# Moving layer 0's modulation vectors from the vector engines to TensorE, and packing the weights by block

## The chip, the cores and the metric

The kernel runs on one core of one Trainium2 chip. The metric is device microseconds of a whole launch. Before the change the median of three runs is 1066.75 us (1066.24 to 1068.56).

## The reference, cut to what matters

The model is a two-layer trunk for 256 tokens of 1024 features, all in float32. Every layer has three sub-layers: a feed-forward network (FFN), a token mixer, and a second FFN. Before each of them the input is modulated by a shift and a scale, and the output of each is weighted by a gate. These nine vectors per layer come from one conditioning vector by a matrix-vector product:

```python
cond = jax.nn.silu(c)                       # (1, 1024)
for l in range(DEPTH):                      # 2 layers
    mod = cond @ ada_w[l] + ada_b[l]        # ada_w[l]: 1024 x 9216, 36 MiB
    sh1, sc1, gt1, sh2, sc2, gt2, sh3, sc3, gt3 = jnp.split(mod, N_MOD, axis=-1)
    f1 = swiglu(modulate(x, sh1, sc1), ffn1_w1[l], ffn1_w3[l], ffn1_w2[l])
    x = layer_norm(DEEPNORM_ALPHA * x + MACARON_HALF * gt1[:, None, :] * f1, ln_g[l, 0], ln_b[l, 0])
    m = token_mixer(modulate(x, sh2, sc2), ...)      # LRU, retention, state-space heads
    x = layer_norm(DEEPNORM_ALPHA * x + gt2[:, None, :] * m, ln_g[l, 1], ln_b[l, 1])
    f2 = swiglu(modulate(x, sh3, sc3), ffn2_w1[l], ffn2_w3[l], ffn2_w2[l])
    x = layer_norm(DEEPNORM_ALPHA * x + MACARON_HALF * gt3[:, None, :] * f2, ln_g[l, 2], ln_b[l, 2])
```

`modulate` is `x * (1 + scale) + shift`; an FFN has w1 and w3 of 1024 x 2816 and w2 of 2816 x 1024.

## The kernel before, in words

**Matrix products.** Every weight block is loaded in float32 into one of three `raw` buffers (128 x 2048). ScalarE (ACT) rounds a half of it, 128 x 1024, to the reduced form fp32r (`wh`), VectorE (DVE) subtracts to get what was lost (`wl`), and the activations are split likewise (`xTh`, `xTl`). A product is then three fp32r matmuls (`mm3`): high by high, high by low, low by high. There are 8 `wh` and 8 `wl` buffers.

**Modulation vectors before.** A vector pair or quadruple is made by `ada_group`. Each item of it loads two chunks of `ada_w` (128 x 1024, rows of 4 KiB) into `s4` buffers, which the profile shows as `s_slot`. One chunk is multiplied by a condition column and added on DVE in one instruction (`scalar_tensor_tensor` in `add_cond`); the other is scaled on ACT and added by DVE. After the last item DVE adds both sums, PE transposes them and DVE reduces over the partitions. Layer 0's vectors 2 to 5 are made in the background of its first FFN, 6 and 7 (`late`) at that FFN's end and the mixer's start. Vector 8 and the vectors of layer 1 come later, in the same manner.

**The start.** `begin` makes the first two vectors (shift 1 and scale 1) together with the first FFN's first columns, in four sections of 256 features. A section loads its part of `ada_w` in pieces of 128 x 4 x 256 (rows of 1 KiB), 256 columns of x, and weights of w1 and w3. DVE and ACT do the 16 multiply-adds of 128 x 256 (`G_SHARE` of them on ACT with an add on DVE), PE transposes the result, DVE and ACT modulate x into `xTh` and `xTl`, and PE does 36 matmuls of 512 columns for the section. Two of a section's three pieces of weights are recorded together with the next section (`LATE`).

**What sets the order.** Nothing is in program order. `Scheduler` records all operations, gives each an estimated duration (`cost`) and a latest start (`place_late`), and places them by list scheduling (`run`), each engine in one fixed order. DMA loads are all issued by SP, also in one fixed order, so that a load waits behind those ahead of it when their buffer is not yet free. The profile shows one source line for all instructions (the one that emits them), so tiles tell them apart. Operations within `sch.fused()` stay together: in the mixer, `y_mm` uses it for four matmuls of 32 output columns each, which go to the four column tiles of the array and stand in the profile as `r_slot<-s_slot,CT`. Each such float32 matmul stands in the trace as two records; an fp32r matmul stands as one.

**Stages.** By the layer norms' statistics in the trace, layer 0's first FFN ends at 225.1 us, its mixer at 357.7, its second FFN at 548.4; layer 1's at 748.5, 870.4 and 1055.5.

Of the kernel before, what the change touches and what calls it, by code (L numbers as in the profile page):

```python
# [66 lines left out]

FFN_SLOTS = 21
# [6 lines left out]
SMB = 8  # L75
# [127 lines left out]
class Scheduler:  # L203
# [156 lines left out]
    def cost(self, eng, m, a, k, out, ins, n, fs, scal, psum, op):  # L360
        if eng == E_SPQ:
# [4 lines left out]
            op.nbytes = nb if run >= 512 else max(2 * nb, nb // run * 157)  # L366
# [286 lines left out]
def trunk_kernel(ctx: ExitStack, tc: tile.TileContext, a: dict, cst: bass.AP, out: bass.AP):  # L653
# [46 lines left out]
    cond = {n: cp.tile([128, KD * n], F32, name=f"cond{n}") for n in (1, 2, 4)}  # L700
    hpi = cp.tile([128, 1], F32, name="hpi")
# [67 lines left out]
    def rows_k(w, r0, r1, c0, c1):  # L769
        return w[r0:r1, c0:c1].rearrange("(k p) f -> p k f", p=128)  # L770

    def piece(w, r0, r1, c0, c1, nm, eng=None, by_cols=False):
        merge = "p k i f -> p k (i f)" if by_cols else "p i k f -> p (i k) f"
        p = Piece((r1 - r0) // 128, c1 - c0, lambda raw: [(raw.rearrange(merge), rows_k(w, r0, r1, c0, c1))], nm, by_cols)
        for i in range(2):
            p.convert(i, eng or V)
        return p
# [44 lines left out]
    def ada_group(vecs, ring=False):  # L822
# [49 lines left out]
        def gate_row(l, j):  # L872
            pt = bank(f"gtt{l}_{j}")
            PE.transpose(pt[0:32, 0:128], modFM[:, l, j:j + 4, :].rearrange("p j k -> p (j k)"), ident)
            row = small([32, 128], f"gtr{l}_{j}")
            S.mul(row, pt[0:32, 0:128], 1.0 if j == 5 else 0.5)
            gtd[l, j // 3] = dp.tile([D], F32, name=f"gtd{l}_{j}")
            SP.dma_start(gtd[l, j // 3].rearrange("(k p) -> k p", p=128), row[0:8, :])

        return [lambda q=q: item(q) for q in range(4 * n)]  # L880
# [110 lines left out]
    def ffn(l, s, nxt, last_features, bg, todo, start=None, late=None):  # L991
        w1, w3, w2 = [a[f"ffn{1 if s == 0 else 2}_{n}"][l] for n in ("w1", "w3", "w2")]
# [311 lines left out]
    def mixer(l, P, nxt, last_features, bg):  # L1304
        win, wout = a["mix_w_in"][l], a["mix_w_out"][l]
# [424 lines left out]
    G_SHARE = [4, 5, 5, 5]  # L1730

    def begin(hs):
        w1, w3 = a["ffn1_w1"][0], a["ffn1_w3"][0]
# [4 lines left out]
        cond_columns(1)  # L1738
        ada_bias_transpose()
# [3 lines left out]
        for n, (k0, nk) in enumerate(SECTIONS):  # L1743
            f0, f1 = k0 * 128, (k0 + nk) * 128
            raws = []
            for j in range(2):
                for q in range(2):
                    raw = t4([128, 4, f1 - f0], f"adaf{n}{j}{q}")
                    SP.dma_start(raw, rows_k(a["ada_w"][0], q * 512, q * 512 + 512, j * D + f0, j * D + f1))
                    raws += [raw[:, k, :] for k in range(4)]  # L1750
# [65 lines left out]
        for n in (2, 4):  # L1816
            cond_columns(n)
# [65 lines left out]
```

## Time and profile before

| | us |
|---|---|
| median of 3 runs | 1066.75 |
| the profiled execution | 1063.61 |
| its span | 1061.8 |
| PE busy | 989.6 (93%) |
| DVE busy | 898.2 (85%) |
| ACT busy | 571.4 (54%) |
| DMA moved | 260.85 MB, 246 GB/s over the span |

The profile shows one execution. A stretch is read by the busy time of each engine in it: an engine that is busy for the whole stretch bounds it, and where none is, the wait that ends last does. A matmul's duration runs from its issue to its end and overlaps with the next one's, so the cost of one on PE is the distance between two starts, not the duration. PEclk is the granted share of TensorE's clock: 1.00 is 2.4 GHz and 0.50 is 1.2 GHz.

### The profile page before, as it was taken

The numbers are of one execution on the slowest core, as the hardware profiler recorded it, in microseconds if no ns is written. First come the engines' busy times: TensorE is split into PE (matmuls) and PEld (weight loads), VectorE is DVE, ScalarE is ACT, GpSimd is POOL, SyncE is SP. The second block draws the span as 40 slices with busy tenths as digits, with TensorE's granted clock in tenths as the row PEclk, the third lists the DMA queues.
The fourth block names the chain that finished last, engine by engine and source line by source line (L and its number), as shares of the span: only waits on it lengthen the run. The fifth ranks groups of instructions, "written<-read, shape, count | busy, mean of one in ns | idle before, by whom it ended". The sixth has DMA issues, their size and how long they took to land. (4 is left out here: it accounts for less than half of the span.)

```text
span 1061.8 us, 16775 instructions
## 1 busy us (share of the span) xinstructions
PE 989.6 (93%) x6617; PEld 887.0 (84%) x6617; DVE 898.2 (85%) x1391; ACT 571.4 (54%) x739; POOL 34.8 (3%) x46
## 2 busy tenths in 40 slices
PE   4899999988699899999989989999998799999996
PEld 3688998978588699899968979998897578999995
DVE  7988999999999999999899996556999898555555
ACT  4676765554376565665556544443546655444440
POOL 0000000010001100000000000000000110000000
PEclk9999999989899999999999999999999899999999
DMA  9999999978138699999969995654460657565521
GB/s 313 313 378 340 348 368 341 334 234 250 41 127 283 227 333 357 381 385 339 335 241 330 328 325 161 199 185 131 137 211 9 229 164 244 189 198 193 180 104 40
DMA packets 159055, 260.85 MB, mean 246 GB/s; under 512 B 14464, under 2 KB 115328, under 8 KB 158976
## 3 DMA queue, kind: packets, MB, share of 16 engines
q1 hardware_dynamic: 158976, 259.77, 71.1%
q8 instruction: 52, 0.85, 0.3%
q14 instruction: 27, 0.22, 0.1%
HBM read 257.10 MB, written 1.07 MB: 243 GB/s over the span
## 5 line engine op out<-in xcount | busy, mean ns | idle before, releaser
L643 ACT CAST wh_slot<-raw_slot 128x1024 fp32r<-128x1024 f32 x320 | 330.8, 1049 | 288.2 <-PE r_slot L643 168.9
L643 DVE TENSOR_TENSOR wl_slot<-raw_slot,wh_slot 128x1024 fp32r<-128x1024 f32 x320 | 386.6, 1221 | 106.9 <-ACT wh_slot L643 105.2
L643 PE MATMUL r_slot<-xTh,wh_slot 128*128 128x256 f32 x1216 | 343.0, 282 | 3.6 <-DVE xTh L643 1.6
L643 PE MATMUL r_slot<-xTl,wh_slot 128*128 128x256 f32 x1216 | 341.5, 281 | 1.3 <-DVE xTl L643 1.2
L643 PE MATMUL r_slot<-xTh,wl_slot 128*128 128x256 f32 x1216 | 341.0, 280 | 0.0
L643 PEld LDWEIGHTS r_slot<-xTh,wh_slot 128*128 128x128 f32 x1216 | 229.6, 189 | 8.0 <-ACT s_slot L643 3.0
L643 PEld LDWEIGHTS r_slot<-xTh,wl_slot 128*128 128x128 f32 x1216 | 232.6, 191 | 0.0
L643 PEld LDWEIGHTS r_slot<-xTl,wh_slot 128*128 128x128 f32 x1216 | 229.8, 189 | 2.7 <-DVE xTl L643 1.7
L643 PE MATMUL r_slot<-wh_slot,g_slot 128*128 128x512 f32 x704 | 224.6, 393 | 0.9 <-DVE g_slot L643 0.9
L643 PE MATMUL r_slot<-wh_slot,xTh 128*128 128x512 f32 (+1 forms) x416 | 148.4, 359 | 11.3 <-DVE xTh L643 4.7
L643 PEld LDWEIGHTS r_slot<-wh_slot,g_slot 128*128 128x128 f32 x704 | 132.3, 189 | 27.3 <-DVE g_slot L643 1.5
L643 DVE TENSOR_TENSOR s_slot<-s_slot,s_slot 128x256 f32<-128x256 f32 (+6 forms) x211 | 147.1, 721 | 8.1 <-ACT s_slot L643 4.7
L643 PE MATMUL r_slot<-wl_slot,xTh 128*128 128x512 f32 (+1 forms) x416 | 146.8, 354 | 3.2 <-DVE wl_slot L643 3.2
L643 PE MATMUL r_slot<-wh_slot,xTl 128*128 128x512 f32 (+1 forms) x416 | 146.0, 353 | 1.6 <-DVE xTl L643 1.4
L643 PE MATMUL r_slot<-wl_slot,g_slot 128*128 128x512 f32 x352 | 138.4, 394 | 0.0
L643 ACT ACTIVATE s_slot<-s_slot,cond 128x1024 f32<-128x1024 f32 (+1 forms) x83 | 82.2, 1002 | 61.8 <-DMA s_slot<-in_ada_w_dram 58.4
L643 PEld LDWEIGHTS r_slot<-wh_slot,xTh 128*128 128x128 f32 x416 | 81.3, 196 | 24.4 <-DVE xTh L643 5.5
L643 DVE SCALAR_TENSOR_TENSOR s_slot<-s_slot,cond,s_slot 128x1024 f32<-128x1024 f32 (+1 forms) x96 | 93.7, 981 | 3.4 <-DMA s_slot<-in_ada_w_dram 3.2
L643 PEld LDWEIGHTS r_slot<-wh_slot,xTl 128*128 128x128 f32 x416 | 81.1, 195 | 14.6 <-DVE xTl L643 4.7
L643 PEld LDWEIGHTS r_slot<-wl_slot,xTh 128*128 128x128 f32 x416 | 81.1, 195 | 13.8 <-DVE wl_slot L643 4.4
L643 DVE TENSOR_TENSOR s_slot<-r_slot,s_slot 128x512 f32<-128x512 f32 x100 | 68.2, 688 | 20.5 <-PE r_slot L643 19.9
L643 PEld LDWEIGHTS r_slot<-wl_slot,g_slot 128*128 128x128 f32 x352 | 66.5, 189 | 12.3
(119 smaller groups left out, 656.8 us busy)
## 6 DMA issues: line engine op xcount, KB each, us to landing
raw_slot<-in_ffn_w_dram SPq DMA_DIRECT2D x126, 1024.0 KB
s_slot<-in_ada_w_dram SPq DMA_DIRECT2D x144, 512.0 KB
raw_slot<-in_mix_w_in_dram SPq DMA_DIRECT2D x20, 1024.0 KB
raw_slot<-in_mix_w_out_dram SPq DMA_DIRECT2D x8, 1024.0 KB
raw_slot<-in_ffn_w_dram SPq DMA_DIRECT2D x12, 512.0 KB
s_slot<-gtd SPq DMA_DIRECT2D x6, 512.0 KB
s_slot<-in_ln_g_dram SPq DMA_DIRECT2D x6, 512.0 KB
s_slot<-in_ln_b_dram SPq DMA_DIRECT2D x6, 512.0 KB
```

The source lines that it names most:

```text
L643: real(*[self.place(v) for v in a], **{n: self.place(v) for n, v in k.items()})
```

## The change: TensorE makes layer 0's vectors 0 to 7, and the host lays the weights out by block

The condition vector is laid 32 times side by side (`condrep`, 128 x 8 x 32), as the stationary operand of one column tile. In `ada_matmul`, which replaces `ada_group` for the vectors 2 to 7 of layer 0, four chunks of `ada_w` are one fused item of 16 float32 matmuls: for each of the four chunks, four of 256 columns, one on each column tile. Two items make a vector. ACT then copies the sums from PSUM, PE transposes them twice and DVE adds the bias. In `begin`, a section's 16 multiply-adds become eight float32 matmuls of 512 columns, on four column tiles, two deep; the four tiles hold different quarters of the contraction dimension and are added up by the reduction that stood there before. Vector 8 of layer 0 and all of layer 1's stay on DVE and ACT.

The host copies w1, w3, w2, the mixer's input and output weights, and the start's part of `ada_w` into one array, in which each block stands as it lies in the buffer: each partition's row is one run of 4 or 8 KiB. Before, a block of w1, w3 or the mixer's input weights had rows of 1 or 2 KiB, and one of w2 or the output weights rows of 4 KiB. The other loads of `ada_w` are as before, rows of 4 KiB. The planner's cost takes 6% off for runs of 4 KiB and more, and there are 6 instead of 8 small buffers (`SMB`).

```diff
+def _blocks():
...
+            if l == 0 and i == 1:
+                f0 = 1024
+                for n in range(4):
+                    for q in range(4):
+                        out.append([("ada_w", 0, q * 256 + k * 128, q * 256 + k * 128 + 128, j * D + n * 256, j * D + n * 256 + 256)
+                                    for k in range(2) for j in range(2)])
+                    out.append([(w, 0, n * 256, n * 256 + 256, 0, 512) for w in (w1, w3)])
+                    out.append([(w1, 0, n * 256, n * 256 + 256, 512, 1024)])
...
-SMB = 8
+SMB = 6
...
-            op.nbytes = nb if run >= 512 else max(2 * nb, nb // run * 157)
+            op.nbytes = nb * (0.94 if run >= 4096 else 1) if run >= 512 else max(2 * nb, nb // run * 157)
...
+    condrep = cp.tile([128, KD, 32], F32, name="condrep")
...
-    def rows_k(w, r0, r1, c0, c1):
-        return w[r0:r1, c0:c1].rearrange("(k p) f -> p k f", p=128)
+    where, _ = _packed()
+
+    def block(*parts):
+        n = sum((r1 - r0) * (c1 - c0) for _, _, r0, r1, c0, c1 in parts) // 128
+        return a["pack"][where[parts]:where[parts] + 128 * n].rearrange("(p f) -> p f", p=128)
...
+    def ada_matmul(l, j):
+
+        nm = f"{l}_{j}"
+        raws = []
+        box = {}
+
+        def item(q):
+            for k in range(2):
+                raws.append(t4([128, D], f"adaw{nm}_{2 * q + k}"))
+                SP.dma_start(raws[-1], a["ada_w"][l, (2 * q + k) * 128:(2 * q + k) * 128 + 128, j * D:j * D + D])
+            if q == 0:
+                box["ps"] = bank(f"adv{nm}")
+            if q % 2:
+                with sch.fused():
+                    for kk in range(2 * q - 2, 2 * q + 2):
+                        for b in range(4):
+                            PE.matmul(box["ps"][32 * b:32 * b + 32, 0:256], condrep[:, kk, :],
+                                      raws[kk][:, 256 * b:256 * b + 256], start=(kk == 0), stop=(kk == 7))
+            if q == 3:
+                fin()
+
+        def fin():
+            ev = t2([128, 256], f"adev{nm}")
+            S.copy(ev, box["ps"][:, 0:256])
+            pt = bank(f"adas{nm}")
+            for h in range(2):
+                PE.transpose(pt[:, h * 128:h * 128 + 128], ev[:, h * 128:h * 128 + 128], ident)
+            V.tensor_tensor(modFM[:, l, j, :].rearrange("p (b h) -> p b h", h=2),
+                            pt[:, 0:256].rearrange("p (h b r) -> p b h r", b=4, r=32)[:, :, :, 0],
+                            abT[:, l, 8 * j:8 * j + 8].rearrange("p (b h) -> p b h", h=2), op=ALU.add)
...
+        V.tensor_copy(condrep, cond[1].rearrange("p (k o) -> p k o", o=1).to_broadcast([128, KD, 32]))
...
-            for kk in range(G_SHARE[n]):
-                add_cond(acg, raws[kk], cond[1][:, kk:kk + 1], kk == 0, False)
...
-            V.tensor_tensor(acc[:, 0, :], acc[:, 0, :], acg, op=ALU.add)
+            pv = bank(f"adv{n}")
+            for h in range(2):
+                with sch.fused():
+                    for b in range(4):
+                        PE.matmul(pv[32 * b:32 * b + 32, :], condrep[:, 2 * b + h, :], raws[2 * b + h],
+                                  start=(h == 0), stop=(h == 1))
+            ev = t2([128, 512], f"adev{n}")
+            S.copy(ev, pv)
...
-                bg = Background(attach(ada([(0, 2), (0, 3), (0, 4), (0, 5)]), extra), 5)
+                bg = Background(attach(adam((0, 2), (0, 3), (0, 4), (0, 5)), extra), 5)
...
-            late = Background([] if l else ada([(0, 6), (0, 7)]), 3)
+            late = Background([] if l else adam((0, 6), (0, 7)), 3)
```

Since the scheduler solves the whole program anew, the order moves in most places. On DVE at the start, ahead of the first section's products, the program had the multiply-adds of the section (`s_slot_95<-s_slot_85,cond_135`), the first of which are these, behind the last step of the conditioning vector:

```order
L643 TENSOR_SCALAR sm_slot_112<-sm_slot_111 8x128
L643 TENSOR_SCALAR s_slot_95<-s_slot_85,cond_135 128x256
L643 SCALAR_TENSOR_TENSOR s_slot_95<-s_slot_85,cond_135,s_slot_95 128x256
L643 TENSOR_SCALAR s_slot_95<-s_slot_84,cond_135 128x256
L643 SCALAR_TENSOR_TENSOR s_slot_95<-s_slot_85,cond_135,s_slot_95 128x256
L643 SCALAR_TENSOR_TENSOR s_slot_95<-s_slot_84,cond_135,s_slot_95 128x256
```

In the changed program the same place on DVE holds the copy into `condrep`, then at once the weights' low parts and the reduction:

```order
L694 TENSOR_SCALAR sm_slot_111<-sm_slot_110 8x128
L694 COPY condrep<-cond_133 128x256
L694 TENSOR_TENSOR wl_slot_74<-raw_slot_63,wh_slot_66 128x1024
L694 TENSOR_TENSOR wl_slot_75<-raw_slot_63,wh_slot_67 128x1024
L694 TENSOR_REDUCE modFM<-r_slot_129 128x2x2
```

All multiply-adds have left DVE there, and the section's reduction follows the weights directly. On PE the end of layer 0's first FFN and the start of its mixer looked so before: transposes of the normalised tokens (`cs,x_res`), then the mixer's first matmuls, whose moving operand `xTh` is made from them:

```order
L643 MATMUL r_slot_129<-cs,modFM 32x128
L643 MATMUL r_slot_128<-cs,x_res 128x128 x4
L643 MATMUL r_slot_127<-cs,x_res 128x128 x4
L643 MATMUL r_slot_126<-wh_slot_69,xTh 128x256
L643 MATMUL r_slot_126<-wl_slot_76,xTh 128x256
```

In the changed program, PE has this at the same place:

```order
L694 MATMUL r_slot_125<-cs,x_res 128x128 x2
L694 MATMUL r_slot_128<-cs,s_slot_98 128x128 x2
L694 MATMUL r_slot_125<-cs,x_res 128x128 x2
L694 MATMUL r_slot_124<-cs,s_slot_97 128x128 x2
L694 MATMUL r_slot_131<-s_slot_89,condrep 32x256 x4
L694 MATMUL r_slot_131<-s_slot_92,condrep 32x256 x4
L694 MATMUL r_slot_131<-s_slot_87,condrep 32x256 x4
L694 MATMUL r_slot_131<-s_slot_86,condrep 32x256 x4
L694 MATMUL r_slot_129<-wh_slot_69,xTh 128x256
```

The first item of vector 7 now stands between the transposes and the matmuls that need their result; its second item stands at the like place for the second half of the tokens. The ten items of vectors 2 to 6 stand earlier, between matmuls of the FFN, as this one does (the `g_slot` rows are the FFN's second product, the `xTh,wh_slot` rows its first):

```order
L694 MATMUL r_slot_131<-wh_slot_73,g_slot_106 128x512
L694 MATMUL r_slot_127<-wh_slot_73,g_slot_104 128x512
L694 MATMUL r_slot_125<-s_slot_86,condrep 32x256 x4
L694 MATMUL r_slot_125<-s_slot_82,condrep 32x256 x4
L694 MATMUL r_slot_125<-s_slot_89,condrep 32x256 x4
L694 MATMUL r_slot_125<-s_slot_92,condrep 32x256 x4
L694 MATMUL r_slot_124<-xTh,wh_slot_66 128x256
```

An item is 16 matmuls in a row, and nothing of the FFN stands between them.

## Rows read from the trace of the kernel before

**Rows 1.** The page: PE's busy time, share of the span, instructions.

```profile
PE 989.6 (93%) x6617; PEld 887.0 (84%) x6617; DVE 898.2 (85%) x1391; ACT 571.4 (54%) x739; POOL 34.8 (3%) x46
```

**Rows 2.** Stretches: length, busy us of each engine, PEclk, DMA share, GB/s.

```profile
0.00:17.90 17.90, 2.79 (x11) 1.90 (x11) 11.20 (x30) 6.93 (x15) 2.11 (x10) 1.00 0.91 287
17.90:62.00 44.10, 41.08 (x175) 31.12 (x176) 40.59 (x93) 27.95 (x49) 0.31 (x1) 1.00 0.98 331
62.00:150.00 88.00, 87.98 (x583) 80.41 (x582) 81.42 (x137) 61.61 (x78) 1.81 (x5) 1.00 1.01 357
225.10:357.70 132.60, 112.31 (x810) 98.58 (x810) 127.47 (x239) 71.76 (x103) 9.40 (x7) 0.93 0.53 175
748.50:870.40 121.90, 108.30 (x782) 94.66 (x781) 117.04 (x222) 67.28 (x98) 6.99 (x6) 0.96 0.46 153
```

**Rows 3.** Timeline of PE around a four-tile group: start, us, what, count.

```profile
303.98 0.28 PE L643 MATMUL r_slot<-wh_slot,xTh 128*128 128x256 f32 x1
304.19 0.42 PE L643 MATMUL r_slot<-s_slot,CT 128*32 128x128 f32 x8
304.54 0.55 PE L643 MATMUL r_slot<-cs,s_slot 128*128 128x128 f32 x3
```

**Rows 4.** Timeline of PE: float32 matmuls over the whole array, 256 columns.

```profile
294.27 1.89 PE L643 MATMUL r_slot<-s_slot,gates 128*128 128x256 f32 x8
```

**Rows 5.** DVE by instruction form, 62 to 245 us: count, busy, mean ns.

```profile
L643 DVE TENSOR_TENSOR s_slot<-s_slot,s_slot 128x1024 f32<-128x1024 f32 x24 | 29.3, 1220 | 0.7 <-ACT s_slot L643 0.6
L643 DVE SCALAR_TENSOR_TENSOR s_slot<-s_slot,cond,s_slot 128x1024 f32<-128x1024 f32 x22 | 28.9, 1315 | 0.0
```

**Rows 6.** The same view, 225 to 241 us.

```profile
L643 DVE TENSOR_TENSOR s_slot<-s_slot,s_slot 128x1024 f32<-128x1024 f32 x4 | 4.9, 1219 | 0.0
...
L643 DVE SCALAR_TENSOR_TENSOR s_slot<-s_slot,cond,s_slot 128x1024 f32<-128x1024 f32 x2 | 2.6, 1278 | 0.0
```

**Rows 7.** Timeline of PE at the start; in brackets, the wait before.

```profile
19.77 0.63 PE L643 MATMUL r_slot<-wl_slot,xTh 128*128 128x512 f32 x1
20.20 0.63 PE L643 MATMUL r_slot<-wh_slot,xTl 128*128 128x512 f32 x1
...
22.60 0.39 PE L643 MATMUL r_slot<-wh_slot,xTh 128*128 128x512 f32 x1
22.83 0.39 PE L643 MATMUL r_slot<-wl_slot,xTh 128*128 128x512 f32 x1
...
34.70 0.49 PE L643 MATMUL r_slot<-wl_slot,xTh 128*128 128x512 f32 x1 [1.28 <-DVE wl_slot L643]
```

**Rows 8.** Timeline of PE: three waits in FFN, mixer 0 and layer 1.

```profile
171.99 0.63 PE L643 MATMUL r_slot<-cs,s_slot 128*128 128x128 f32 x4 [2.36 <-DVE s_slot L643]
...
285.36 0.65 PE L643 MATMUL r_slot<-s_slot,CT 128*32 128x128 f32 x8 [8.19 <-DVE s_slot L643]
...
628.69 0.44 PE L643 MATMUL r_slot<-cs,s_slot 128*128 128x128 f32 x2 [3.53 <-ACT B L643]
```

**Rows 9.** Stretches, columns as in rows 2, where the clock fell.

```profile
172.60:176.00 3.40, 3.40 (x12) 2.73 (x11) 2.14 (x4) 1.04 (x1) 0.00 (x0) 0.50 1.07 361
223.80:237.40 13.60, 11.06 (x69) 10.62 (x68) 12.72 (x22) 6.28 (x10) 1.57 (x2) 0.75 0.42 144
281.80:292.10 10.30, 5.58 (x40) 4.14 (x41) 10.30 (x20) 4.47 (x9) 0.00 (x0) 0.50 0.01 2
630.00:633.40 3.40, 3.39 (x14) 2.67 (x13) 3.33 (x9) 0.83 (x5) 0.00 (x0) 0.50 0.48 155
```

**Rows 10.** DMA of 80 to 85 us, then of 70 to 75: packets, sizes.

```profile
DMA packets 1735, 1.77 MB, mean 354 GB/s; under 512 B 19, under 2 KB 1731, under 8 KB 1735
...
DMA packets 528, 2.04 MB, mean 407 GB/s; under 512 B 31, under 2 KB 31, under 8 KB 528
```

**Rows 11.** Waits, 62 to 225 us: us in total, times, longest.

```profile
ACT s_slot L643 <- DMA s_slot<-in_ada_w_dram: 9.4, 7, 3.0
```

**Rows 12.** Timeline of ACT before the wait at 628.69 us.

```profile
626.08 1.15 ACT L643 ACTIVATE s_slot<-s_slot,cond 128x1024 f32<-128x1024 f32 x1 [2.65 <-DMA s_slot<-in_ada_w_dram]
```

More of the change, by code (lines that the diff above doesn't have):

```diff
@@ L65, in _consts, with _packed, _pack @@
     return c
+def _blocks():
+    out = []
+    for l in range(L):
+        for i in (1, 2):
+            w1, w3, w2 = [f"ffn{i}_w{n}" for n in (1, 3, 2)]
+            f0 = 512
+            if l == 0 and i == 1:
[6 more added lines that the diff above has]
+                    out.append([(w1, 0, n * 256, n * 256 + 256, 512, 1024)])
+                out += [[(w3, 0, h * 512, h * 512 + 512, 512, 1024)] for h in range(2)]
+            else:
+                out += [[(w, l, h * 512, h * 512 + 512, 0, 512)] for w in (w1, w3) for h in range(2)]
+            for f in range(f0, FF, 256):
+                out += [[(w, l, 0, D, f, f + 256)] for w in (w1, w3)]
+            out += [[(w2, l, f, f + 256, 0, D)] for f in range(0, FF, 256)]
+        out += [[("mix_w_in", l, 0, D, c, c + 256)] for c in range(0, 2560, 256)]
+        out += [[("mix_w_out", l, c, c + 256, 0, D)] for c in range(0, D, 256)]
+    return out
+def _packed():
+    at, n = {}, 0
+    for b in _blocks():
+        at[tuple(b)] = n
+        n += sum((r1 - r0) * (c1 - c0) for _, _, r0, r1, c0, c1 in b)
+    return at, n
+def _pack(inputs):
+    import numpy as np
+    at, n = _packed()
+    buf = np.empty(n, np.float32)
+    for b, o in at.items():
+        parts = []
+        for nm, l, r0, r1, c0, c1 in b:
+            v = np.asarray(inputs[nm])[l, r0:r1, c0:c1]
+            parts.append(v.reshape(-1, 128, c1 - c0).transpose(1, 0, 2).reshape(128, -1))
+        v = np.concatenate(parts, axis=1)
+        buf[o:o + v.size] = v.reshape(-1)
+    return buf
 FFN_SLOTS = 21
@@ new lines, in ada_matmul @@
+    def ada_matmul(l, j):
[25 more added lines that the diff above has]
+                            abT[:, l, 8 * j:8 * j + 8].rearrange("p (b h) -> p b h", h=2), op=ALU.add)
+            if j % 3 == 2:
+                gate_row(l, j)
+        return [lambda q=q: item(q) for q in range(4)]
@@ L882, in ln_of, with gate_row @@
+    def gate_row(l, j):
+        pt = bank(f"gtt{l}_{j}")
+        PE.transpose(pt[0:32, 0:128], modFM[:, l, j:j + 4, :].rearrange("p j k -> p (j k)"), ident)
+        row = small([32, 128], f"gtr{l}_{j}")
+        S.mul(row, pt[0:32, 0:128], 1.0 if j == 5 else 0.5)
+        gtd[l, j // 3] = dp.tile([D], F32, name=f"gtd{l}_{j}")
+        SP.dma_start(gtd[l, j // 3].rearrange("(k p) -> k p", p=128), row[0:8, :])
     def ln_of(l, s):
```

65 lines of the change are left out of this document (25 added, 40 removed).

## The prediction

> **What bounds the kernel now.** The page comes first: PE is busy for 93% of the span and DVE for 85% [rows 1]. The next view is the table by stretches, which tells where the rest is lost. From 62 to 150 us PE is busy for 87.98 of 88.00 us, so whatever is put on PE in layer 0's first FFN is paid in full there. The losses lie elsewhere: 15.1 us before the first products (17.90 - 2.79), 3.0 us in the rest of the start, 20.3 us in layer 0's mixer (132.60 - 112.31) and 13.6 us in layer 1's (121.90 - 108.30). DVE is nearly full at the start and in layer 0's mixer, 40.59 of 44.10 and 127.47 of 132.60 us [rows 2]. So PE bounds the FFNs, and DVE sets PE's waits in the mixers. Third, the timeline of PE shows single waits: 2.36 us in the first FFN and 8.19 us in the mixer, both for DVE, and 3.53 us in layer 1's first FFN for ACT [rows 8]. Fourth, around each of these the clock stands at half, 0.50, after PE had run dry, so that a wait is paid again in the work behind it [rows 9].
>
> The change puts work on the engine that is full and takes it off the one that makes it wait. The question is which of the two is larger.
>
> **What the change adds on PE.** The nearest row is the mixer's group of four column tiles. Its eight records, two for each of four matmuls of 128 columns, start at 304.19 and the next instruction starts at 304.54: 0.35 us. The matmul ahead started 0.21 us earlier, where one of its kind takes 0.12 [rows 3]; so about 0.09 us goes to entering the tiled form. Four matmuls of 128 columns one after the other, at the price of the whole-array float32 row, would take longer: there eight records of 256 columns take 1.89 us with the last one's tail of 0.4, or 0.215 each [rows 4], so eight of 128 columns 0.86 us. The 0.35 us say that the tiles run side by side. I split it as two times 0.107 (half of 0.215) of streaming, 0.04 for the starts and 0.10 for leaving.
>
> For the new sizes that gives, by estimate: four matmuls of 256 columns are two records deep, 2 x 0.215 + 0.03 = 0.46 us; an item is four of them and one entry and exit, 1.84 + 0.19 = 2.03 us; a vector is two items, 4.06 us; six vectors 24.4 us. Four of 512 columns are 2 x 0.43 + 0.03 = 0.89 us, and a section of the start has two of them, 1.97 us with its entry and exit. The low bound is streaming alone, 1.72 us an item. The high bound is one tile after the other, 16 x 0.43 = 6.9 us an item. I take 2.03, since rows 3 show this very form.
>
> Where it lands: the ten items of vectors 2 to 6 stand in the FFN's full stretch, +20.3 us. Vector 7's two items stand where PE waits for the mixer's features: the stretch from 223.8 to 237.4 has 2.5 us of idle PE [rows 9], and there is more just before it. I count them at nothing; without that cover they cost 4.1. The first section's matmuls run while PE has nothing else (rows 2, first row), the other three cost 3 x 1.97 = +5.9. PE has four transposes fewer, -0.4. The sum of the costs is 25.8 us.
>
> **What it takes off.** DVE loses 29.3 + 28.9 us of full-width adds and multiply-adds [rows 5] and about 16 multiply-adds per section at the start. That counts only where PE waits.
>
> - The start: DVE's low part of the weights is late once by 1.28 us. The first products also run at half rate: their starts are 0.43 us apart (19.77 to 20.20) and later 0.23 (22.60 to 22.83) [rows 7]. That is ten or eleven matmuls too slow by 0.2 us, 2.3 us in all. With four sections' matmuls ahead of or between them PE is busy sooner. I take both, -3.6, from bounds of 0 and -6. The first products themselves I leave at 17.9: the adds leave DVE, but a copy from PSUM and 3.5 us of tiled matmuls at half clock come in.
> - The wait at 171.99 is for a transposed sum of modulations, and goes: -2.4, and the 3.4 us at half clock behind it [rows 9], -1.7. Together -4.1; 0 if another late step takes its place.
> - The features' stretch, 223.8 to 237.4, has half its time at half clock: 11.06 busy us, so about 5.5 at half rate, -2.7 if PE is kept busy by vector 7.
> - The mixer: from 225 to 241 us DVE still does 4.9 + 2.6 = 7.5 us of modulations [rows 6], while the mixer's own chain on DVE has begun; PE's wait of 8.19 us at 285.36 is at the end of that chain [rows 8]. DVE has no gap in between, so -7.5. Of the 10.3 us at half clock there PE works 5.6 [rows 9], -2.8.
> - The loads: rows of 1 KiB move at 354 GB/s, with 1731 of 1735 packets under 2 KB, and rows of 4 KiB at 407 with 31 of 528 [rows 10]. A load of 1.05 MB then takes 2.58 us for 2.96. In the FFNs that is hidden. In a mixer some four loads stand in line with what waits for them, -1.5 us each mixer, -3.0; bounds 0 and, with all 14 loads of a mixer, -5.3 each.
> - The wait at 628.69: ACT waited 2.65 us for modulation weights and so was late with the mixer's coefficients [rows 12], for which PE waited 3.53 us. With shorter loads ahead in the queue I expect this late load in time: -3.5, and the 3.4 us at half clock, -1.7 [rows 9]. Together -5.2, bounds 0 and that.
>
> The Trainium skill speaks against the last two: its page "DMA: Bandwidth & Descriptors", section Specifications, gives 512 B as the least transfer for full line rate, so that rows of 1 KiB would already be served at the full rate. Rows 10 differ from it by 15%, and the measurement decides. By the page the packing would bring nothing: the sum would be 8.2 us higher.
>
> **The sum.** 25.8 - 3.6 - 4.1 - 2.7 - 10.3 - 3.0 - 5.2 = -3.1 us on the profiled execution's 1063.6 us (span 1061.8 and 1.8 around it). That execution was 3.1 us under the median of the runs, so I carry the difference over to the median: 1066.75 - 3.1, about 1064 us.
>
> **The rivals.**
>
> 1. *PE pays and DVE's time does not come back*, slower. In the mixer of layer 1 no modulations are made, and PE still idles for 13.6 us there [rows 2]: the waits may be the mixer's own chain, in which one step waits for the next whatever DVE does beside it. The place is the wait at 285; the point from which it decides is that this wait keeps more than 5 of its 8 us. Then the mixer's 10.3 us and, since a new plan makes its own late steps, the 4.1 and the 3.6 stay: +14.9 us, 1082; with half of them back 1073. Against it: the layer 0 mixer is 10.7 us longer than layer 1's, about what I take off.
> 2. *The loads bind more than PE's row shows*, faster still. The start is served at 331 GB/s with the DMA engines at 98% [rows 2], 14.6 MB in 44.1 us; at 407 GB/s these are 35.9. If the sections wait for loads, the start gains up to 8 us more: 1056. Against it: from 22.60 on PE's starts at the start are 0.23 us apart, with few gaps.
> 3. *The packing brings nothing*, slower: the sum without its 8.2 us is +5.1, 1072. This is what the skill's 512 B would make of it.
> 4. *PE waits for modulation weights in its fixed order*, slower. ACT waited seven times, 9.4 us in all, for them from 62 to 225 us [rows 11]; these loads now release PE. All of that on PE: +9.4 on the sum, 1073. Against it: the loads ahead of them become shorter, and the items on PE push the FFN back.
> 5. *The tiles do not run side by side*: (6.9 - 2.03) x 12 items is 58 us, and 16 us for the start by the same ratio; about 1138. Rows 3 all but exclude it.
>
> **How the numbers follow.** The forecast, 1064, has a chance of 0.42 with its own range of 1057 to 1069; rival 1 has 0.26, rival 2 0.14, rival 3 0.08, rival 4 0.06, rival 5 0.02, and 0.02 are left for a new order that happens to cost or gain. The bound for no change is 0.2%, 2.1 us, about what can be told by measurement. Of the forecast's 0.42, 0.30 lie under 1064.6 and 0.12 within the bound; rival 2 is faster. So faster is 0.44. Within the bound lie 0.12, and 0.09 from rivals 1, 3 and the rest: 0.21. Slower is what remains, 0.35. The range reaches to rival 2 and past it by the unknown of the start, 1052, and over most of rival 1, to 1080.
>
> **What would show it.** In the new profile, an item on PE (sixteen matmuls on `condrep`) should take 2.0 us to the next FFN matmul, with no wait for DMA ahead of it, and the first FFN should end some 15 us later than 225. The first products should start near 18 us. The wait before the mixer's first tiled group should be 1 us or less, with the clock at 1.00, and that mixer about 120 us long in place of 132.6. Stretches of weight loads should run near 400 GB/s, and the wait for ACT's coefficients in layer 1's first FFN should be gone. If the first FFN is longer by 20 us or more and the mixer keeps its wait, rival 1 is right; if the first products come well before 17 us or the FFN ends no later than 230, rival 2 is.

## The result, and the profile after

The changed kernel takes 1071.61 us (median of 20 runs, 1066.32 to 1080.49), the kernel before 1066.38 (20 runs, 1062.00 to 1071.26). The ratio is 1.0056, with a 95% interval of 1.0036 to 1.0076: slower by about half a per cent, where 0.3% faster was forecast. The profiled execution took 1069.99 us, its span is 1068.2 us. The first part of its page stands against [rows 1]:

```profile
PE 1013.8 (95%) x7061; PEld 896.3 (84%) x7061; DVE 826.3 (77%) x1276; ACT 541.2 (51%) x705; POOL 32.4 (3%) x46
```

PE is busy for 24.2 us more and idle for 17.8 us less (54.4 of 1068.2 us, before 72.2 of 1061.8): together the 6.4 us by which the span grew. The 24.2 us are net: they hold what the change put on PE, less what PE saved where its clock no longer stood at half, so they are not the forecast's bill of 25.8 by themselves (that is read from single items below). Where the time is lost, the table by stretches tells; its columns are those of [rows 2]. First the changed kernel, a stage to a row from 62 us on, with the first FFN in two:

```profile
0.00:17.90 17.90, 5.98 (x32) 2.71 (x33) 5.27 (x13) 6.19 (x11) 2.11 (x10) 1.00 0.88 336
17.90:62.00 44.10, 43.19 (x225) 31.42 (x223) 25.91 (x43) 26.55 (x37) 0.31 (x1) 1.00 0.97 381
62.00:150.00 88.00, 88.00 (x664) 76.20 (x663) 58.27 (x143) 44.56 (x66) 1.01 (x5) 1.00 0.88 320
150.00:239.00 89.00, 89.00 (x736) 75.27 (x735) 51.14 (x81) 37.05 (x53) 1.81 (x4) 1.00 0.78 292
239.00:361.50 122.50, 112.57 (x836) 97.28 (x836) 117.70 (x228) 70.40 (x101) 8.20 (x6) 0.94 0.53 186
361.50:549.90 188.40, 186.66 (x1259) 170.91 (x1258) 184.36 (x222) 115.64 (x136) 2.81 (x6) 1.00 0.93 352
549.90:744.40 194.50, 190.74 (x1294) 175.00 (x1293) 145.99 (x201) 96.35 (x120) 5.88 (x5) 1.00 0.64 228
744.40:874.30 129.90, 114.08 (x802) 98.68 (x801) 123.02 (x223) 67.61 (x100) 7.01 (x6) 0.93 0.42 145
874.30:1061.20 186.90, 183.61 (x1225) 168.87 (x1225) 110.92 (x124) 76.85 (x88) 2.39 (x2) 0.99 0.48 166
```

And of the kernel before the three stages that [rows 2] leave out:

```profile
357.70:548.40 190.70, 186.86 (x1259) 170.32 (x1258) 180.80 (x219) 113.74 (x133) 3.12 (x6) 1.00 0.95 339
548.40:748.50 200.10, 196.46 (x1314) 178.28 (x1314) 153.40 (x206) 99.26 (x123) 4.15 (x5) 0.98 0.68 229
870.40:1055.00 184.60, 182.41 (x1228) 167.86 (x1226) 109.41 (x123) 77.72 (x89) 2.39 (x2) 1.00 0.51 169
```

Here and below a stage reaches from the start of one stage's last BATCH_NORM_STATS2 on DVE to that of the next. How far the changed kernel is behind at each stage's end, beside what the prediction's terms add up to at that point:

| at the end of | before, us | after, us | behind by | forecast |
|---|---|---|---|---|
| layer 0, first FFN | 225.1 | 239.0 | +13.9 | +15.4 (25.8 - 3.6 - 4.1 - 2.7) |
| layer 0, mixer | 357.7 | 361.5 | +3.8 | +3.6 (-10.3 - 1.5) |
| layer 0, second FFN | 548.4 | 549.9 | +1.5 | +3.6 |
| layer 1, first FFN | 748.5 | 744.4 | -4.1 | -1.6 (-5.2) |
| layer 1, mixer | 870.4 | 874.3 | +3.9 | -3.1 (-1.5) |
| layer 1, second FFN | 1055.0 | 1061.2 | +6.2 | -3.1 |

Up to layer 1's mixer the sum of the forecast is met or beaten, and at that point the changed kernel is ahead. Of the 4.1 us some 2.4 are work that moved over the line: the FFN has 20 PE instructions fewer (1294 for 1314), the mixer 20 more (802 for 782), about 0.12 us each. Then layer 1's mixer and last FFN, in which no operation was changed, lose 10.3 us, those 2.4 included.

In the mixer PE idles for 15.8 us (129.90 - 114.08) where it idled for 13.6. Part of the rest lies in this place of the changed kernel, on PE's timeline (start, us, what, count; in brackets the wait before):

```profile
816.68 0.55 PE L694 MATMUL r_slot<-cs,s_slot 128*128 128x128 f32 x3 [1.62 <-DVE ti_slot L694]
817.79 7.25 PE L694 MATMUL r_slot<-s_slot,s_slot 128*128 128x128 f32 x30 [0.57 <-ACT s_slot L694]
824.97 0.58 PE L694 MATMUL r_slot<-wh_slot,xTh 128*128 128x256 f32 x1
```

and by stretches, before and behind the first of these waits:

```profile
814.80:818.20 3.40, 1.21 (x7) 0.60 (x5) 3.19 (x13) 3.37 (x9) 0.00 (x0) 1.00 0.00 0
818.20:831.90 13.70, 13.25 (x89) 10.70 (x89) 11.87 (x18) 8.25 (x14) 0.52 (x2) 0.50 0.24 78
```

PE ran nearly dry from 814.8 to 818.2, the clock fell to half, and the retention's float32 matmuls, which the new order puts there in one block of 30 records, ran at half clock, 0.24 us each. In the kernel before, records of the same tiles and also of 128 columns stand at full clock, with weight products right behind them:

```profile
815.95 2.83 PE L643 MATMUL r_slot<-s_slot,s_slot 64*128 64x128 f32 x20 [0.15 <-ACT s_slot L643]
818.71 0.39 PE L643 MATMUL r_slot<-wh_slot,xTh 128*128 128x256 f32 x1
```

There 20 records take 2.83 us, 0.14 each. How much of the loss is this block's, e13 and e11 tell below.

### The profile page after: what moved, and what is told of

Its sections match the earlier page's. It is cut to its first block, busy times and chain, and to the rows that moved or that the text cites. A ratio compares the mean times of both kernels' runs of the same rounds, so it can differ in the third digit from the quotient of the medians.

```text
span 1068.2 us, 17515 instructions
## 1 busy us (share of the span) xinstructions
PE 1013.8 (95%) x7061; PEld 896.3 (84%) x7061; DVE 826.3 (77%) x1276; ACT 541.2 (51%) x705; POOL 32.4 (3%) x46
## 4 chain that ended last, share of the span: by engine, by line
PE 51%; DVE 18%; DMA 4%; issue 2%; ACT 2%; POOL 0%; DVEq 0%; ACTq 0%; SPq 0%
PE r_slot L694 51%; DVE s_slot L694 9%; DVE wl_slot L694 5%; DMA s_slot<-in_ada_w_dram 3%; DVE x_res L694 2%; DMA raw_slot<-in_pack_dram 1%; DVE ti_slot L694 1%; ACT s_slot L694 1%; DVE xTl L694 1%; ACT wh_slot L694 0%; POOL ti_slot L694 0%; DVE xTh L694 0%; ACT xTh L694 0%; ACT L694 0%; ACT B L694 0%
## 5 line engine op out<-in xcount | busy, mean ns | idle before, releaser
L694 PE MATMUL r_slot<-wh_slot,xTh 128*128 128x512 f32 (+1 forms) x416 | 145.8, 354 | 11.7 <-DVE s_slot L694 4.6
L694 PEld LDWEIGHTS r_slot<-wh_slot,g_slot 128*128 128x128 f32 x704 | 131.7, 188 | 26.6 <-ACT g_slot L694 0.4
L694 PE MATMUL r_slot<-wl_slot,xTh 128*128 128x512 f32 (+1 forms) x416 | 143.5, 348 | 1.9 <-DVE wl_slot L694 1.9
L694 DVE TENSOR_TENSOR s_slot<-s_slot,s_slot 128x256 f32<-128x256 f32 (+10 forms) x168 | 110.1, 677 | 7.7 <-ACT s_slot L694 3.9
L694 PEld LDWEIGHTS r_slot<-wh_slot,xTl 128*128 128x128 f32 x416 | 79.8, 193 | 17.9 <-DVE xTl L694 4.6
L694 ACT ACTIVATE s_slot<-s_slot,cond 128x1024 f32<-128x1024 f32 x40 | 46.1, 1152 | 63.2 <-DMA s_slot<-in_ada_w_dram 63.0
L694 DVE SCALAR_TENSOR_TENSOR s_slot<-s_slot,cond,s_slot 128x1024 f32<-128x1024 f32 x37 | 47.2, 1276 | 1.2 <-DMA s_slot<-in_ada_w_dram 1.2
```

What stands on the lines that cost most here:

```text
L694: real(*[self.place(v) for v in a], **{n: self.place(v) for n, v in k.items()})
```

## The experiments

Theory A: the order that the scheduler found for layer 1 costs the time. Theory B: something that the change leaves behind in layer 1 (packed loads, fewer small buffers, earlier arrival) costs it, whatever the order. Theory C: PE's bill outweighs what is saved. D and E, on where an item on PE pays, came with the mixed kernel. Stage lengths are of the one profiled execution, which lies between 4.5 us under its run's median (e5) and 6.6 us over it (e2); the ratio is that to the kernel before, run beside it, with its 95% interval:

| run | median us | ratio | FFN, mixer, FFN of layer 0 | of layer 1 |
|---|---|---|---|---|
| before | 1066.4 | 1 | 225.1, 132.6, 190.7 | 200.1, 121.9, 184.6 |
| the change | 1071.6 | 1.0056 (1.0036 to 1.0076) | 239.0, 122.5, 188.4 | 194.5, 129.9, 186.9 |
| e1, price 60 | 1067.8 | 1.0023 (1.0006 to 1.0039) | 238.8, 121.4, 193.4 | 201.8, 119.4, 184.7 |
| e2, price 101 | 1072.2 | 1.0046 (1.0023 to 1.0070) | 238.8, 130.1, 194.5 | 199.3, 122.3, 185.1 |
| e3, unpacked | 1074.5 | 1.0080 (1.0055 to 1.0106) | 238.6, 122.5, 191.9 | 195.6, 128.6, 186.9 |
| e4, before, slack 5400 | 1079.0 | 1.0115 (1.0084 to 1.0146) | 223.9, 144.3, 194.7 | 190.9, 130.2, 186.3 |
| e5, mixed | 1061.2 | 0.9947 (0.9921 to 0.9973) | 228.2, 126.2, 187.8 | 194.8, 125.8, 185.1 |
| e6, mixed, other order | 1074.6 | 1.0068 (1.0041 to 1.0094) | 225.9, 134.0, 194.7 | 193.9, 129.1, 185.8 |
| e7, DVE work back | 1079.4 | 1.0117 (1.0080 to 1.0154) | 239.0, 129.5, 188.6 | 195.5, 131.8, 186.9 |
| e8, before, slack 5000 | 1059.4 | 0.9926 (0.9902 to 0.9950) | 222.1, 132.5, 191.3 | 194.6, 125.3, 185.1 |
| e9, before, packed | 1061.7 | 0.9966 (0.9948 to 0.9984) | 223.2, 131.7, 189.1 | 199.5, 122.5, 184.7 |
| e10, e8 packed | 1058.5 | 0.9933 (0.9910 to 0.9956) | 222.1, 131.2, 190.7 | 193.2, 125.6, 185.1 |
| e11, change, slack 5400 | 1074.8 | 1.0085 (1.0058 to 1.0112) | 239.2, 124.2, 188.9 | 195.6, 131.2, 186.9 |
| e12, change, slack 5000 | 1082.7 | 1.0162 (1.0133 to 1.0192) | 239.6, 127.3, 192.6 | 201.8, 132.7, 185.2 |
| e13, before's order in layer 1 | 1064.5 | 0.9996 (0.9979 to 1.0012) | 239.0, 121.9, 188.4 | 198.0, 124.7, 184.0 |
| e14, before with the change's | 1075.4 | 1.0095 (1.0068 to 1.0122) | 224.4, 132.0, 191.6 | 199.1, 133.9, 187.1 |
| e15, e13 with slack 9000 | 1066.5 | 1.0014 (1.0000 to 1.0029) | 239.4, 122.5, 189.0 | 202.6, 124.1, 184.7 |
| e16, e5 with before's layer 1 | 1060.4 | 0.9951 (0.9933 to 0.9968) | 227.5, 126.4, 191.1 | 196.1, 125.6, 184.7 |

**Other prices, other orders (e1, e2).**

```diff
-            c = 27
+            c = 60        # e1; e2: c = 101 and SETTINGS = [(7000, 5000)]
```

> One number is changed: the scheduler's price of every further matmul in a fused item, 27 ns to 60. The work, the loads and the buffers stay; the scheduler solves anew and so gives another order everywhere. Theory A (order): the 8.0 us that layer 1's mixer lost (129.9 us for 121.9) come from the order that the scheduler happened to find there, in stages whose work the change doesn't touch; in this order that mixer is 118 to 124 us long and the whole 6 to 9 us shorter than the changed kernel, 1062 to 1066. Theory B (resources): something that the change leaves behind in layer 1 (bursts of packed loads, fewer small buffers) makes that mixer longer whatever the order: it stays at 127 to 132 us and the whole at 1069 to 1074. Theory C (PE's bill alone): the 26 us on PE were never to be won back; the whole stays at 1069 to 1074 with gains and losses spread over all stages.

> The same price set to 101 ns, which makes an item 1.95 us, as the trace after shows it, and the scheduler's look-ahead length from 7900 to 7000 and slack from 5800 to 5000, for another order once more. Theory A: layer 1's mixer 117 to 124 us, the whole 1061 to 1067. Theory B: that mixer 127 to 132 us, the whole 1068 to 1074. Theory C: 1068 to 1074 with the mixer at any length. If A holds in both runs and the two wholes differ by more than 2 us, the order is worth more than the change itself.

In both, layer 1's mixer is back at 119.4 and 122.3 us, as theory A has it and B has not. But the wholes are longer than A expected (1067.8 and 1072.2), and e2's lies where theory C has it: each order loses in another place, e1 in the two FFNs between, e2 in these and in layer 0's mixer. The first FFN is 238.8 us in both: PE's bill doesn't hang on the order.

**Packing (e3, and e9, e10 below).**

```diff
-            op.nbytes = nb * (0.94 if run >= 4096 else 1) if run >= 512 else max(2 * nb, nb // run * 157)
+            x0 = ins[0].ap_ if isinstance(ins[0], VT) else ins[0]
+            flat = str(x0.tensor.name).startswith(("in_ffn", "in_mix"))
+            op.nbytes = nb * (0.94 if run >= 4096 or flat else 1) if run >= 512 else max(2 * nb, nb // run * 157)
...
-                  lambda raw: [(raw.rearrange("p a b c -> p (a b c)"), block((*w, r0, r1, c0, c1)))], nm, by_cols)
+                  lambda raw: [(raw.rearrange("p k i f -> p k (i f)" if by_cols else "p i k f -> p (i k) f"),
+                                a[w[0]][w[1]][r0:r1, c0:c1].rearrange("(k p) f -> p k f", p=128))], nm, by_cols)
```

> The changed kernel in its own order, instruction for instruction on every engine, but the weights of the FFNs and mixers are loaded from the arrays as they come, in rows of 1 to 2 KiB as before (the blocks of the start, and with them layer 0's first sections, stay packed). By the prediction's term for the loads (3.0 us in the two mixers and 5.2 at the wait of layer 1's first FFN) the whole is 4 to 8 us longer than the changed kernel, 1075 to 1080, with waits for wh_slot and wl_slot in the mixers. By the rival that packing brings nothing: 1070 to 1073, within 0.2% of the changed kernel. By theory B, that the packed loads' bursts cost layer 1's mixer its time: that mixer 121 to 125 us and the whole 1064 to 1068.

The first lines keep the scheduler's price of a load, and so its order. The run takes 2.9 us more, between the two expectations; the intervals of this run and of the change overlap, so the size alone is not sure. Theory B's bursts are out (mixer 128.6).

**The kernel before in other orders (e4, e8).** `SETTINGS = [(7900, 5400)]` and `[(7900, 5000)]`.

> The kernel before with nothing changed but the scheduler's slack, 5800 to 5400: the same work, loads and buffers in another order. Theory A: the time moves by more than 0.4% (over 4 us) from the kernel before, and most of it lies in stages that both share, the mixers first. Theories B and C: the order is worth little, within 0.2% of the kernel before.

> The kernel before with the scheduler's slack at 5000, a third order of the same work. If the kernel before stands in a lucky order, this one is again slower than it, by 0.2 to 1.2% (1069 to 1079); if the order with slack 5400 was an unlucky one, it is within 0.2%.

The same work takes 1079.0, 1066.4 or 1059.4 us; in e4 it is the mixers that are longer, by 11.7 and 8.3 us, and layer 1's first FFN that is shorter, by 9.2. That an order is worth over 4 us is shown; that before's was a lucky one is not: the third is faster by 0.74%.

**Vectors 2 to 5 back on DVE (e5, e6).**

```diff
-   bg = Background(attach(adam((0, 2), (0, 3), (0, 4), (0, 5)), extra), 5)
+   bg = Background(attach(ada([(0, 2), (0, 3), (0, 4), (0, 5)]), extra), 5)
...
-        if not first and out.shape[0] == 32:
-            c = 27
+        if (len(op.calls) - 1) % 4 and out.shape[0] == 32:
+            c = 20
```

> The changed kernel with vectors 2 to 5 of layer 0 back on DVE and ACT, as before the change; the start's sections and vectors 6 and 7 stay on TensorE, all loads stay packed, and the scheduler prices a fused item by its fours (the first of four in full, 20 ns for the others: 1.97 us an item, as traced) with look-ahead 7000 and slack 5000. Theory D (place decides): an item on PE costs its full 1.95 us in the first FFN, where PE is never idle, and pays where PE waits. Eight items leave PE there, 15.6 us; DVE, busy for 109 of the 177 us from 62 to 239, has room for the 39 us that they take on it (two thirds of 58). First FFN 222 to 227 us for 239, layer 0's mixer still 120 to 126, the whole 1052 to 1062, faster than both. Theory E (DVE's relief in the FFN is what shortens the mixer): with DVE loaded again the mixer goes back to 130 or more, and the whole stays at 1064 to 1070.

> The same kernel with look-ahead 7900 and slack 6200, for another order. Theory D: first FFN again 222 to 227 us; the whole within 6 us of the other order, 1052 to 1066. Theory E: as there, 1064 to 1072. The distance between the two orders says how far a gain of this size stands clear of the order.

The first FFN fell by 10.8 and 13.1 us of the 15.6 (e5's misses its range by 1.2): DVE is loaded again, and PE idles there for 5.3 us in e5 (160.91 busy of 166.20). The mixer gave back 3.7 and 11.5. e5 is 0.5% faster than the kernel before, e6, with the same work, 0.7% slower, outside both expectations.

**DVE's share of the mixer's chain (e7).**

```diff
+   if bn >= 4 and n < 27 and self.ops[x].eng == E_DVE:      # bn: bn_stats so far
+       for _ in range(3):
+           self.spare_op()                                  # add of 128x192 on a tile of its own
+       n += 3
```

> The changed kernel in its own order, with 27 adds of 128x192 on a tile of their own put on DVE, three behind each of the nine instructions that follow the end of layer 0's first FFN: about 0.27 us each, 7.3 us in all, as much as the modulations took there before. The forecast's step (DVE's modulations stand in the mixer's chain): layer 0's mixer 128 to 133 us for 122.5, the whole 1077 to 1083. Rival 1 (the mixer's waits are its own chain, whatever DVE does beside it): mixer 121 to 125, the whole 1070 to 1074.

The tile's own view gives count and duration (ns, least, median, most):

```profile
L762 DVE TENSOR_TENSOR spare<-spare x27: 341/358/359, 239.6 to 252.3; 128x192 f32<-128x192 f32 x27
```

They took 9.6 us instead of 7.3; the mixer is 7.0 us longer and the whole 7.8 (6.5 by the ratios). So work on DVE at this place is on the path, as the forecast's step has it and rival 1 has not. But the delay doesn't return at the wait that the forecast named. Before a tiled group of the mixer PE waits for 1.01 us at most; the longest new wait comes earlier, for the normalised tokens, which DVE finishes later:

```profile
246.93 1.11 PE L695 MATMUL r_slot<-cs,x_res 128*128 128x128 f32 x4 [4.62 <-DVE x_res L695]
...
302.26 0.42 PE L695 MATMUL r_slot<-s_slot,CT 128*32 128x128 f32 x8 [1.01 <-DVE s_slot L695]
```

Of the 7.0 us 5.1 are idle time of PE; for the other 1.9 it is busy for longer, at a mean clock of 0.92 for 0.94.

**Packing alone (e9, e10).** The block loads of e3's diff the other way round, in the kernel before.

> One part of the change alone: the kernel before in its own order, instruction for instruction, with the weights of the FFNs and mixers loaded from packed blocks; all modulations stay on DVE and ACT, and the start's first sections stay unpacked. By the prediction's terms (3.0 us in the mixers, and the late modulation weights behind PE's wait at 628.69 in time, 5.2): 1057 to 1060, with that wait gone. By what the reverse did in the changed kernel's order (2.9 us): 1062 to 1065, the wait at 628.69 shorter at most. By the rival that packing brings nothing: 1065 to 1068.

> The same packing in the order with slack 5000, which alone gave 1059.4 us. If packing and order add up, 1055 to 1058, under every version so far; if the loads did not bind in that order, 1058 to 1061.

e9 gains 0.34%, 3.6 us (1061.7, just under the 1062 to 1065 that e3 let expect); e10 gains nothing beside e8. PE's wait for ACT's coefficients is nearly as long as in [rows 8], with ACT again kept by modulation weights (PE's, then ACT's timeline of e9):

```profile
623.91 0.69 PE L694 MATMUL r_slot<-cs,s_slot 128*128 128x128 f32 x2 [3.18 <-ACT B L694]
```

```profile
621.30 1.15 ACT L694 ACTIVATE s_slot<-s_slot,cond 128x1024 f32<-128x1024 f32 x1 [2.89 <-DMA s_slot<-in_ada_w_dram]
```

**The change at the same slacks (e11, e12).** `SETTINGS` as in e4 and e8.

> The changed kernel with the scheduler's slack at 5400, under which the kernel before took 1079.0. If an order is good or bad by its slack, this one is slow too, 1080 to 1086; if every solution is its own draw, it lies anywhere from 1064 to 1080. First FFN 237 to 240 us in any order, since PE is full there.

> The changed kernel with slack 5000, under which the kernel before took 1059.4: 1062 to 1066 if the order is good by its slack, anywhere from 1064 to 1080 if not. With the three slacks on both sides, 5800, 5400 and 5000, the change by itself is the mean of three differences: theory C (PE's bill against the losses it saves nearly even) says between -3 and +5 us, with single differences beyond 8 us of either sign.

The first FFN is as expected in both. The difference to the kernel before at equal slack is +0.56, -0.30 and +2.36%: the slack makes no order good or bad, and e12's 1082.7 lies above both of its ranges. The mean, +0.9% or 9 us, misses theory C's -3 to +5. Three draws that lie so far apart do not settle it.

**Layer 1's order exchanged (e13, e14), and two versions from it (e15, e16).**

```diff
         self.restore(best[1])
+        self.pin(best[0], 0)
+
+    def pin(self, span, slack):
...
+        for o in self.ops:
+            o.prio = o.start - span
...
+            j, p, e = map(int, x.split(":"))
+            o = self.ops[j]
+            o.prio = p
+            if o.alts:
+                o.alts, o.pref, o.pdur = {e: o.alts[e]}, e, o.alts[e][1]
+        self.run(span, slack)
```

The lines left out read, for the operations `j` of the last stages, the start time `p` in the other kernel and the engine `e`.

> The changed kernel in its own order up to the end of layer 0's second FFN, and from there on in the order of the kernel before (the scheduler is handed the start times that it had found there as priorities; TensorE's rows of layer 1 then agree with those of before in 3032 of 3068). From that stage's end to the last BN_STATS the kernel before took 506.6 us and the changed one 511.3. Theory A (order): that stretch falls to 505 to 508 us and the whole by 4 to 6, to 1065 to 1068. Theory B (something that the change leaves behind in layer 1): the stretch stays at 510 to 513 and the whole at 1070 to 1073.

> The reverse: the kernel before, unpacked loads and all, in its own order up to layer 1's first FFN, and from some 50 us into that stage on in the order that the changed kernel has there. Theory A: the stretch from the end of layer 0's second FFN to the last BN_STATS grows from 506.6 to 510 to 515 us, with layer 1's mixer at 127 to 132, and the whole to 1070 to 1075. Theory B: 505 to 508 us, the whole within 0.2% of the kernel before.

> As the first of these, but with slack 9000 in the last solution, so that the scheduler departs from the given order where that lets an engine start sooner. Theory A: 502 to 507 us for the stretch, the whole 1061 to 1067. Theory B: as there, 1069 to 1073.

> The faster of the two mixed kernels (vectors 2 to 5 on DVE, the rest on TensorE), which took 505.7 us from the end of layer 0's second FFN to the last BN_STATS, with the kernel before's order there. Theory A: since that stretch is already as short as before's (506.6), the whole stays within 3 us of its 1061. A gain of more than that would say that before's order is better than the stretch's length shows.

With before's order in layer 1 alone the changed kernel takes 1064.5 us, 7 less (6.4 by the ratios; 4 to 6 were expected), and the stretch is 506.7 us (198.0 + 124.7 + 184.0). The kernel before takes 1075.4 with the changed kernel's, nearly 10 more (the stretch is 520.1 us and its mixer 133.9, both more than expected), and the block of 30 records comes with it, at half clock (PE's timeline, then the stretch):

```profile
822.65 7.69 PE L659 MATMUL r_slot<-s_slot,s_slot 128*128 128x128 f32 x30 [0.57 <-ACT s_slot L659]
```

```profile
822.90:833.10 10.20, 10.20 (x44) 9.31 (x44) 7.43 (x10) 5.79 (x10) 0.10 (x1) 0.50 0.28 104
```

That is theory A, both ways; B is out, since the kernel before has none of what B names. With before's order in layer 1 on both sides nothing is left for theory C either (0.9996); with the changed kernel's on both (the change against e14, 1.0056 against 1.0095) the change is even ahead by some 4 us, though these two intervals overlap. Theory C's question is open only for the order of layer 0, which was not pinned.

What it is in the order that costs the time is shown in part only. The half clock alone it is not: in e13 the clock stands at half for 13.7 us of this mixer too (its stretch and its mixer come first), and e11, another order of the changed kernel, has the block of 30 records and a longer mixer than the change, at a mean clock of 0.97 (its mixer, then PE's timeline):

```profile
833.50:847.20 13.70, 9.51 (x21) 6.55 (x22) 12.47 (x18) 7.09 (x11) 3.11 (x1) 0.50 0.57 204
747.30:872.00 124.70, 110.52 (x792) 95.77 (x790) 118.13 (x222) 70.40 (x101) 6.91 (x6) 0.93 0.44 156
```

```profile
747.90:879.10 131.20, 112.05 (x803) 94.77 (x801) 123.06 (x224) 66.58 (x99) 7.02 (x6) 0.97 0.42 143
```

```profile
821.54 6.05 PE L694 MATMUL r_slot<-s_slot,s_slot 128*128 128x128 f32 x30 [0.57 <-ACT s_slot L694]
```

Over layer 1's mixer and last FFN together the change takes 8.1 us more than e13. PE idles for 3.5 of them (19.1 us for 15.6) and is busy for 4.6 more. Of the 4.6 an estimated 1.9 come from the stretches at half clock, in which PE worked for 13.25 us instead of 9.51. The idle time is spread over late steps of DVE, of which these are the longest in the change; e13 has other ones, up to 3.43 us:

```profile
793.72 0.38 PE L694 MATMUL r_slot<-wh_slot,xTh 128*128 128x256 f32 x1 [2.38 <-DVE s_slot L694]
...
872.63 0.50 PE L694 MATMUL r_slot<-wl_slot,xTh 128*128 128x512 f32 x1 [1.42 <-DVE wl_slot L694]
...
875.62 0.50 PE L694 MATMUL r_slot<-wh_slot,xTl 128*128 128x512 f32 x1 [2.49 <-DVE xTl L694]
```

e15's freer order gains nothing over e13 (stretch 511.4 us, its range missed, in an execution 4.6 us over the run's median). e16 stays within 1 us of e5, as A expected. The fastest versions are e10 and e8 (1058.5 and 1059.4), the kernel before in another order, with and without packing; e16, e5 and e9 (1060.4, 1061.2, 1061.7) beat both kernels too.

## Why the prediction was wrong

**The step that failed** is "0.02 are left for a new order that happens to cost or gain". The prediction let layer 1's mixer and last FFN stand as they were but for 1.5 us of loads, because no operation in them changes. But the scheduler orders the whole program anew, and its order of layer 1 cost 7 us (e13 against the change) to 10 us (e14 against before). A draw of one per cent either way (1059 to 1079 us for the kernel before in three orders) is larger than the sum of -3.1. It was no mechanism of the change, and so had to stand in the range and the chances as a term of its own. With before's order in layer 1 the changed kernel is at 1064.5 us and the forecast was 1064; but against a kernel before of 1065.8 that is no change (0.9996), so by this pair the sum was some 2.7 us too good as well; the pair of the change and e14 (some -4 us) would bear it out. The term of the sum that did not come is that of the wait at 628.69, below.

**PE's bill: right.** An item on PE's timeline, between matmuls that otherwise start 0.12 us apart:

```profile
164.88 0.28 PE L694 MATMUL r_slot<-xTl,wh_slot 128*128 128x256 f32 x1
165.09 1.93 PE L694 MATMUL r_slot<-s_slot,condrep 128*32 128x256 f32 x32
166.96 0.38 PE L694 MATMUL r_slot<-xTh,wl_slot 128*128 128x256 f32 x1
167.18 0.28 PE L694 MATMUL r_slot<-xTh,wh_slot 128*128 128x256 f32 x1
```

1.87 us to the next start, 0.09 before it for entering and 0.10 behind the next matmul: 2.06 for 2.03; the tiles run side by side (not rival 5). PE did not wait once from 62 to 239 us (177.00 busy of 177.00), so rival 4 is out too, and the FFN paid in full.

**The start: even.** The first products start at 16.84 us, 1.1 earlier than in [rows 2]; they stand 0.23 us apart from the second on, where [rows 7] have 0.43; and from 17.9 to 62 us PE idles for 0.9 us instead of 3.0. With the 2.3 us for the half rate that makes 5.5 us of gain for the 3.6, against a bill of three sections at some 2 us each (1.86 to the next start), 6. Rival 2's 8 us more did not come.

```profile
16.84 0.50 PE L694 MATMUL r_slot<-wh_slot,xTh 128*128 128x512 f32 x1 [1.90 <-DVE xTh L694]
17.18 0.40 PE L694 MATMUL r_slot<-wl_slot,xTh 128*128 128x512 f32 x1
17.41 0.39 PE L694 MATMUL r_slot<-wh_slot,xTh 128*128 128x512 f32 x1
```

**The clock and the wait at 172: right.** From 17.9 us to the first FFN's end the clock stands at 1.00. The features' stretch, 223.8 to 237.4 and at 0.75 in [rows 9], now begins with the mixer's first matmuls at 237.4 us, and in it PE is busy throughout at full clock:

```profile
237.70:251.30 13.60, 13.60 (x132) 12.30 (x132) 11.93 (x26) 6.29 (x11) 1.47 (x1) 1.00 0.59 223
```

**Layer 0's mixer: right in size.** 122.5 us for 132.6, where "about 120" was forecast; the 8.19 us of [rows 8] have become two waits:

```profile
286.00 0.39 PE L694 MATMUL r_slot<-wh_slot,xTh 128*128 128x256 f32 x1 [1.64 <-DVE s_slot L694]
...
294.67 0.43 PE L694 MATMUL r_slot<-s_slot,CT 128*32 128x128 f32 x8 [1.46 <-DVE s_slot L694]
```

So rival 1's sign, a wait that keeps more than 5 of its 8 us, did not come. That the wait went because the modulations left DVE is argued, not shown: e7's work on DVE delays the mixer at another wait. That the mixer gains holds in every order tried: it takes 121.4 to 130.1 us in the five orders of the changed kernel (the change, e1, e2, e11, e12) and 132.5 to 144.3 in the three of the kernel before. The 10 us at half clock stayed, though, at another place, from 309.6 to 319.9 us with PE at work:

```profile
309.60:319.90 10.30, 9.83 (x69) 7.53 (x69) 9.28 (x15) 7.73 (x14) 0.52 (x2) 0.50 0.32 108
```

**The loads: size right, place wrong.** 3.0 us were put into the mixers. Packing is worth 3.6 us (e9), 2.9 (e3, its interval overlapping) or nothing (e10), and in e9's profile it is the FFNs, where the prediction held the loads to be hidden, that are shorter, by 1.9 and 1.6 us in layer 0; the mixers change by -0.9 and +0.6. In e3 layer 0's second FFN is 3.5 us longer than in the change, and both mixers are not. So the 2.3 us by which that FFN was shorter in the change, and which were not forecast, go with the packing by both of these runs. Rows do move faster: the start's stretch moved 331 GB/s in [rows 2] and 332 in e9, where its blocks are not packed, but 381 in the change, with the DMA engines at 97 to 98% in all three (near 400 was forecast). The Trainium skill ("DMA: Bandwidth & Descriptors", Specifications) would have rows of 1 KiB at the full rate already; the trace does not agree. Rival 3 is out in before's order, by e9; in the order with slack 5000 (e10) it holds.

**The wait at 628.69: wrong.** It was to vanish. In e9 3.18 us of 3.53 remain, and in the changed kernel three waits add up to 3.8:

```profile
625.57 0.53 PE L694 MATMUL r_slot<-cs,s_slot 128*96 128x128 f32 x3 [1.88 <-DVE s_slot L694]
...
628.60 0.44 PE L694 MATMUL r_slot<-cs,s_slot 128*128 128x128 f32 x2 [1.34 <-ACT B L694]
...
635.14 0.39 PE L694 MATMUL r_slot<-xTh,wh_slot 128*128 128x256 f32 x1 [0.54 <-ACT B L694]
```

Shorter loads ahead do not bring the modulation weights in time. That FFN was shorter all the same, by 5.6 us, which hid the miss; with before's order there (e13) it is shorter by 2.1, so most of the gain was the new order's luck.

**What stays open:** which waits of an order make layer 1 longer or shorter, and whether the change would win or lose without the order's draw. Over the five orders tried it took 1067.8 to 1082.7, and before, over three, 1059.4 to 1079.0; the ranges overlap.

## What to carry to other kernels

Where a scheduler orders a program anew, compare the order in the stages that the change does not touch, and give its draw a term of its own: run the kernel before in two or three orders first, since a change worth less than their spread can't be judged from one order of each. Hold the order fixed (pin it, or put work in at emission) when one part's worth is to be measured. Work moved onto a full engine is paid in full (2.06 us an item for 2.03 forecast); what it frees elsewhere counts only at the places where that engine waits.

## What the runs showed of the hardware

- The clock can stay at half although TensorE works: for 13.7 us with PE busy for 13.25 of them in layer 1's mixer, and for 10.2 us with PE busy throughout in e14, both mostly on float32 matmuls of 128 columns, behind 3.4 us in which PE was busy for 1.2. Other drops ended after 3.4 us with PE as busy, such as those of [rows 9] at 172.6 and 630.0. The Trainium skill ("TensorE: Matmul & The Clock Gate", What's actually happening) has the clock return after a spell of sustained work; by PE's busy time these two stretches do not follow it.
- A float32 add of 128x192 on DVE takes 0.36 us, where 0.27 had been expected and 192 of the 1024 columns of [rows 5] would come to 0.23: many small instructions cost more than their columns.
- Executions of one order differ, in some orders by more than the effects in question: the changed kernel's 20 by 14 us, e8's eight by 2. In the changed kernel the fastest execution has a mean granted clock of 0.983 and the slowest 0.970.
